# Four unused pieces of SBUF that shift the matmul operands' tiles by 128 to 192 bytes

## The chip, the cores and the metric

The kernel runs on one core of one Trainium2 chip. The metric is the device time of one execution in microseconds (us), the median of several. An execution runs one program on five engines, each with its own instruction stream: TensorE (PE in the profile; its weight loads are listed apart as PEld), VectorE (DVE), ScalarE (ACT), GpSimd (POOL) and SyncE (SP), with DMA queues that move data between device memory and SBUF. SBUF holds 128 partitions; a tile takes the same bytes, from the same start address, in each of them. A matmul reads two SBUF tiles: the weights (a block of 128 columns, loaded into the array by LDWEIGHTS) and the moving operand (up to 512 columns, streamed by MATMUL), and adds into PSUM.

## The reference, cut to what matters

A decoder trunk of two layers on 512 positions of width 1024, in float32. Layer 0 mixes with a Conformer convolution module, layer 1 with sparse attention (16 heads of 64, compressed, selected and windowed branches); each mixer is followed by a SwiGLU FFN of inner width 2816.

```
x = x + conformer_conv_module(rmsnorm(x, norm_mix[0]), ...)
x = x + swiglu_ffn(rmsnorm(x, norm_ffn[0]), ffn_w_in[0], ffn_w_out[0])
x = x + nsa_attention(rmsnorm(x, norm_mix[1]), ...)
x = x + swiglu_ffn(rmsnorm(x, norm_ffn[1]), ffn_w_in[1], ffn_w_out[1])

def swiglu_ffn(h, w_in, w_out):
    gate, up = jnp.split(h @ w_in, 2, axis=-1)
    return (jax.nn.silu(gate) * up) @ w_out
```

## The kernel before

All activations are kept transposed: eight tiles x[0..7] of 128 channels by 512 positions. Precision is kept by splitting every operand in two float32r tiles, a high part (names ending in h: hh, wh, sh, oh, ah) and the remainder (hl, wl, sl, ol, al); a product is then three matmuls, high x high, high x low and low x high.

**Projections.** `proj_start` and `proj_tile` (L396, L430) compute a tile of 128 output channels for all 512 positions: 8 blocks of the inner dimension x 3 matmuls = 24 matmuls of 512 columns, one after the other (mm3, L319 to L322; L438 to L440 where the order is fixed; the convolution's own tiles at L596). Moving operands are hh and hl (the normed input), a (the convolution's activations) or oh and ol (the attention's output); weights are wh and wl, split by ScalarE (L246) and VectorE (L268) from a raw tile wr that a DMA brought.

**FFN, first half.** The first 4 of 22 inner tiles are plain projections. The other 18 are computed in `pair` (L1200) by a scheme with seven half-size products for a 2x2 block of gate and up, in place of eight: `operand` (L1068) prepares seven combinations of the input's halves, kept split in the tiles bo (4 of them, 256 columns each for high and low), and the weights come as w1 (tiles wh, wl), or as sums in the tiles sh and sl that ScalarE and VectorE write anew in each pair (`s_part`, L1136). A product is 4 blocks; a block is three matmuls of 256 columns, or, where the combination is `WIDE`, one of 512 (high and low of the input side by side) and one of 256. Of the seven products of a pair, in their order, the weights are: wh/wl short (12 matmuls), sh/sl short (12), sh/sl long (8), sh/sl short (12), wh/wl long (8), sh/sl long (8), sh/sl long (8). All go through one line:

```
1155:                 mm = lambda out, a, b, f=False, z=False: pe(
1156:                     nc.tensor.matmul(out, a[:, k], b, start=f, stop=z, skip_group_check=True))
```

**FFN, second half.** The same scheme over the output matrix: moving operands oz, weights wh/wl or, for sums, soh and sol, which stand in the same buffers as wh and wl. The plain part of it streams ah and al.

**Attention.** Projections of q, k and v (v has the weights' columns as the moving operand, 304 or 256 wide, and hh, hl as weights, L1975), scores (L2109, L2110), transposes of the probabilities (L2155, plain float32), values (L2187), output projection.

**What sets addresses.** Tiles are cut from pools, and pools are stacked: those of the left side grow up from the bottom of SBUF, those opened with side="right" grow down from its top. A pool that is opened later starts where the earlier one of its side ends. So the start of every tile follows from the sizes of all pools below it. The pools touched: `hp` (left: hh, hl, and in the FFN the y tiles), `cp` and `ct` (right: everything of the convolution), `sw` (right: sh, sl, r22, S2 and operands' scratch of the FFN; `so`, with S, and `sb`, with bo, lie above it), `op` (right: q and later oh, ol; under it qk and kp with scores' and small tiles).

The order of instructions is partly fixed by the program and partly left to a scheduler that runs when the kernel is built.

Of the kernel before, what the change touches and what calls it, by code (L numbers as in the profile page):

```python
# [10 lines left out]
F32 = mybir.dt.float32  # L11
# [8 lines left out]
P = 128  # L20
# [121 lines left out]
def trunk(ctx: ExitStack, tc: tile.TileContext, A, out):  # L142
# [2 lines left out]
    xp = ctx.enter_context(tc.tile_pool(name="xp", bufs=1))  # L145
    wp = ctx.enter_context(tc.tile_pool(name="wp", bufs=3))
    tp = ctx.enter_context(tc.tile_pool(name="tp", bufs=2))
    hx = [ExitStack()]
    hps = [hx[0].enter_context(tc.tile_pool(name="hp", bufs=1, reuse_waits="tile"))]
    cnt = [0]  # L150

    def nm(s):
        cnt[0] += 1
        return f"{s}_{cnt[0]}"


    units = []
# [166 lines left out]
    def rsqrt(pool, a, rows, n, tag, eng=None):  # L324

        y = pool.tile([rows, n], F32, tag=tag + "y", name=nm("rsy"), bufs=1)
        t = pool.tile([rows, n], F32, tag=tag + "t", name=nm("rst"), bufs=1)
        nc.vector.tensor_scalar(t.bitcast(I32), a.bitcast(I32), 1, None, ALU.logical_shift_right)
        nc.vector.tensor_scalar(y.bitcast(I32), t.bitcast(I32), -1.0, float(0x5F3759DF), ALU.mult, ALU.add)
        for _ in range(3):  # L330
            if eng is nc.gpsimd:
                eng.tensor_tensor(t, y, y, ALU.mult)
                eng.tensor_tensor(t, t, a, ALU.mult)
                eng.tensor_scalar(t, t, -0.5, 1.5, ALU.mult, ALU.add)
                eng.tensor_tensor(y, y, t, ALU.mult)
                continue
            nc.vector.scalar_tensor_tensor(t, y, -0.5, y, ALU.mult, ALU.mult)
            nc.vector.tensor_tensor(t, t, a, ALU.mult)
            state["root"] = nc.vector.scalar_tensor_tensor(y, t, 1.5, y, ALU.add, ALU.mult)
        return y  # L340
# [9 lines left out]
    def split_hi(m, gcol):  # L350
        hh[m] = hps[0].tile([P, T], F32R, tag=f"hh{m}", name=nm(f"hh{m}"))
        parted(nc.scalar.activation(hh[m], x[m], AF.Copy, scale=v(gcol + m)))
# [121 lines left out]

    def conv_module():
        with ExitStack() as cx:
            cp = cx.enter_context(tc.tile_pool(name="cp", bufs=1, side="right"))
            ct = cx.enter_context(tc.tile_pool(name="ct", bufs=2, side="right"))
            pa = cx.enter_context(tc.tile_pool(name="pa", bufs=1, space=PSUM))
# [514 lines left out]
    def ffn(acc, gnext, layer):  # L994
# [9 lines left out]
        with ExitStack() as cx:  # L1004
# [4 lines left out]
            so = cx.enter_context(tc.tile_pool(name="so", bufs=1, side="right", reuse_waits="tile"))  # L1009
            sx = ExitStack()  # L1010
            sb = sx.enter_context(tc.tile_pool(name="sb", bufs=1, side="right", reuse_waits="tile"))
            sw = sx.enter_context(tc.tile_pool(name="sw", bufs=1, side="right", reuse_waits="tile"))
            box = {}

# [462 lines left out]
    def nsa(acc, gnext):  # L1477
        cx = ExitStack()
# [8 lines left out]
        def pool(cxx, name, bufs, **kw):  # L1487
            return cxx.enter_context(tc.tile_pool(name=name, bufs=bufs, **kw))
# [89 lines left out]
        ppx, p2x = ExitStack(), ExitStack()  # L1578
        p2 = pool(p2x, "ap2", 3, space=PSUM, reuse_waits="tile")
        px = pool(ppx, "apx", 4, space=PSUM, reuse_waits="tile")  # L1580
        op = pool(cx, "op", 1, side="right", reuse_waits="tile")
        qx = ExitStack()
        qk = pool(qx, "qk", 1, side="right", reuse_waits="tile")
        sx = ExitStack()
# [762 lines left out]
        return acc  # L2347

    acc = conv_module()
    cx0.close()  # L2350
    acc = ffn(acc, V_NM1, 0)
    acc = nsa(acc, V_NF1)
    ffn(acc, None, 1)
    hx[0].close()

# [155 lines left out]
```

## Time and profile before

| | |
|---|---|
| three runs | 1157.77, 1159.03, 1159.23 us; median 1159.03 |
| profiled execution | 1158.09 us, of which 1156.2 us span from the first to the last instruction |
| granted TensorE clock | 1.000 |
| DMA | 179.69 MB, mean 155 GB/s |

The pair loops of the two FFNs lie at 221.39 to 398.12 and 862.13 to 1038.81 us of the span. A row of the timeline gives start, duration, engine, line, operation, output<-inputs, and how many instructions are merged in it. TensorE's instructions overlap: the next starts before the one ahead ends, so what one costs is the distance of two starts, not its duration.

### The profile page before, as it was taken

Reading aid. Unit: us, or ns where it says so; the run is one execution under the profiler, and the core shown is the slowest. Engines: PE = TensorE matmul, PEld = TensorE weight load, DVE = VectorE, ACT = ScalarE, POOL = GpSimd, SP = SyncE. Lnnn points to the kernel's source line nnn. Section 1 sums busy time; section 2 is a strip of 40 time slices with the busy share of each in tenths; the row PEclk is TensorE's granted clock in tenths of the full one; section 3 lists DMA queues with packets and bytes.
Section 4 is the critical chain, followed back from the end, with each engine's and each line's share of the span. In section 5 each row is a group of like instructions: output and inputs, shape, how many; then the busy total and the mean of one; then the engine's idle time right before and its main releaser. Section 6 shows DMA issues by size and latency. Waiting matters only on the chain.

```text
span 1156.2 us, 20758 instructions
## 1 busy us (share of the span) xinstructions
PE 1148.9 (99%) x7644; PEld 990.5 (86%) x7644; DVE 949.4 (82%) x1878; ACT 639.7 (55%) x1206; POOL 306.4 (26%) x399
## 2 busy tenths in 40 slices
PE   9999999999999999999999999999999999999998
PEld 6878788899999889998779877778889999998998
DVE  6999898999999788874565988855799999987876
ACT  6666654455555454553334788863455555554543
POOL 1698101011111101110233577850001111110120
PEclk9999999999999999999999999999999999999999
DMA  9646437477777768753465211144237777776892
GB/s 361 228 116 190 119 115 214 109 183 191 190 185 192 178 196 212 153 160 91 137 162 153 60 31 36 28 130 126 92 108 176 185 187 184 183 178 169 230 197 83
DMA packets 81269, 179.69 MB, mean 155 GB/s; under 512 B 29200, under 2 KB 31120, under 8 KB 80144
## 3 DMA queue, kind: packets, MB, share of 16 engines
q1 hardware_dynamic: 56928, 105.52, 29.4%
q0 software_dynamic: 23952, 72.59, 28.1%
q8 instruction: 60, 0.98, 0.4%
q14 instruction: 41, 0.34, 0.1%
q10 hardware_dynamic: 288, 0.26, 0.1%
HBM read 163.50 MB, written 4.75 MB: 146 GB/s over the span
## 4 chain that ended last, share of the span: by engine, by line
PE 94%; DVE 3%; ACT 1%; issue 1%; DMA 0%; SPq 0%; ACTq 0%
PE st L1157 43%; PE pp L596 7%; PE pp L320 6%; PE pp L322 6%; PE pp L321 6%; PE O L2187 3%; PE T L2155 3%; PE st L321 2%; PE st L320 2%; PE st L322 2%; PE S L2109 2%; PE pv L1975 1%; PE S L2110 1%; PE pp L440 1%; PE pp L439 1%; PE pp L438 1%
## 5 line engine op out<-in xcount | busy, mean ns | idle before, releaser
L1157 PE MATMUL st<-bo,sh 128*128 128x256 f32 (+1 forms) x1008 | 259.8, 333 | 0.0
L246 ACT ACTIVATE wh<-wr 128x1024 fp32r<-128x1024 f32 (+2 forms) x143 | 148.3, 1038 | 140.6 <-issue 54.0
L268 DVE TENSOR_TENSOR wl<-wr,wh 128x1024 fp32r<-128x1024 f32 (+2 forms) x143 | 177.3, 1240 | 51.3 <-ACT wh L246 47.5
L1157 PE MATMUL st<-bo,sl 128*128 128x256 f32 x720 | 203.2, 282 | 0.0
L1157 PEld LDWEIGHTS st<-bo,sh 128*128 128x128 f32 x1008 | 170.5, 189 | 20.1
L1157 PEld LDWEIGHTS st<-bo,sl 128*128 128x128 f32 x720 | 136.6, 190 | 0.1
L1143 DVE TENSOR_TENSOR sl<-S,sh 128x512 fp32r<-128x512 f32 x144 | 93.1, 687 | 16.9 <-ACT sh L1142 16.6
L1157 PE MATMUL st<-bo,wh 128*128 128x256 f32 (+1 forms) x432 | 103.1, 316 | 0.0
L1157 PE MATMUL st<-oz,soh 128*128 128x256 f32 x512 | 88.7, 278 | 0.0
L1118 POOL DMA_DIRECT2D S<-fw_x x36 | 21.1, 588 | 241.5 <-ACT c L1172 125.8
L1142 ACT ACTIVATE sh<-S 128x512 fp32r<-128x512 f32 x144 | 82.3, 619 | 0.2
L1196 ACT ACTIVATE g<-g 128x512 f32<-128x512 f32 x36 | 22.8, 633 | 106.5 <-DVE g L1193 106.5
L1157 PE MATMUL st<-bo,wl 128*128 128x256 f32 x288 | 80.3, 279 | 0.0
L1124 POOL DMA_DIRECT2D S<-fw_x x36 | 42.6, 1184 | 136.6 <-DMA S<-fw_x 136.5
L1157 PEld LDWEIGHTS st<-oz,soh 128*128 128x128 f32 x512 | 77.9, 188 | 0.5
L320 PE MATMUL pp<-hh,wh 128*128 128x512 f32 x192 | 77.1, 401 | 0.1
L673 POOL TENSOR_TENSOR pv<-pv,tap 128x512 f32<-128x512 f32 x45 | 69.7, 1550 | 26.0 <-ACT tap L670 23.1
L1157 PEld LDWEIGHTS st<-bo,wh 128*128 128x128 f32 x432 | 70.7, 188 | 6.6
L321 PE MATMUL pp<-hl,wh 128*128 128x512 f32 x192 | 75.8, 395 | 0.0
L322 PE MATMUL pp<-hh,wl 128*128 128x512 f32 x192 | 75.7, 395 | 0.0
L2143 POOL TENSOR_SCALAR Pm<-Pm,rq,gates 128x512 f32<-128x512 f32 (+2 forms) x96 | 67.0, 708 | 33.0 <-DVE rq L2133 21.9
L1157 PE MATMUL st<-oz,sol 128*128 128x256 f32 x256 | 71.7, 280 | 0.2
(350 smaller groups left out, 2951.5 us busy)
## 6 DMA issues: line engine op xcount, KB each, us to landing
S<-fw_x POOLq DMA_DIRECT2D x72, 512.0 KB, 5.8
wr<-fw_in SPq DMA_DIRECT2D x44, 512.0 KB
So<-fw_q POOLq DMA_DIRECT2D x38, 512.0 KB, 7.3
wr<-fw_q SPq DMA_DIRECT2D x24, 512.0 KB
bd<-bands POOLq DMA_DIRECT2D x8, 1280.0 KB, 13.0
r<-fw_x SPq DMA_DIRECT2D x36, 256.0 KB
wr<-cw_in SPq DMA_DIRECT2D x14, 512.0 KB
wr<-fw_p SPq DMA_DIRECT2D x12, 512.0 KB
```

What stands on the lines that cost most here:

```text
L246: state["wh"] = parted(after(nc.scalar.activation(hi[:, :cols], raws[i][:, :cols], AF.Copy), pin.get(AF)))
L268: parted(after(nc.vector.tensor_tensor(lo[:, :cols], raws[i][:, :cols], hi[:, :cols], ALU.subtract), pin.get(ALU)))
L320: held(nc.tensor.matmul(ps, wh, xh, start=first, stop=False))
L321: held(nc.tensor.matmul(ps, wh, xl, start=False, stop=False))
L322: held(nc.tensor.matmul(ps, wl, xh, start=False, stop=last))
L596: pe(nc.tensor.matmul(ps, w[:, k * P:(k + 1) * P], z[k], start=m == 0, stop=m == len(todo) - 1))
L673: last["pool"] = pe(nc.gpsimd.tensor_tensor(dst, c, z, ALU.add))
L1124: pe(nc.gpsimd.dma_start(S[n].rearrange("p (a b) -> p a b", a=2), fw_x(n)[:, None, 2 * T:].to_broadcast([P, 2, T]), accum_op=ALU.add))
L1142: pe(nc.scalar.activation(h_[:, c], z, AF.Copy))
L1143: pe(nc.vector.tensor_tensor(l_[:, c], z, h_[:, c], ALU.subtract))
L1157: nc.tensor.matmul(out, a[:, k], b, start=f, stop=z, skip_group_check=True))
L2143: kept(nc.gpsimd.tensor_scalar(Pt, Pt, sm[:, k:k + 1], gates[:, t + k, br * 16 + h:br * 16 + h + 1], ALU.mult, ALU.mult))
```

## The change

A helper `gap` opens a pool with a single tile that nothing reads or writes. Four such pieces are put in: 128 bytes on the left ahead of `hp`, 160 bytes on the right ahead of the convolution's pools, 192 bytes on the right between `sb` and `sw` in the FFN, and 128 bytes on the right ahead of `op` in the attention.

```
+    def gap(cx, n, **kw):
+
+        cx.enter_context(tc.tile_pool(name=nm("gap"), bufs=1, **kw)).tile([P, n // 4], F32, name="gap")
...
-    hps = [hx[0].enter_context(tc.tile_pool(name="hp", bufs=1, reuse_waits="tile"))]
...
+    gap(ctx, 128)
+    hps = [hx[0].enter_context(tc.tile_pool(name="hp", bufs=1, reuse_waits="tile"))]
...
     def conv_module():
         with ExitStack() as cx:
+            gap(cx, 160, side="right")
             cp = cx.enter_context(tc.tile_pool(name="cp", bufs=1, side="right"))
...
             sb = sx.enter_context(tc.tile_pool(name="sb", bufs=1, side="right", reuse_waits="tile"))
+            gap(sx, 192, side="right")
             sw = sx.enter_context(tc.tile_pool(name="sw", bufs=1, side="right", reuse_waits="tile"))
...
+        gap(cx, 128, side="right")
         op = pool(cx, "op", 1, side="right", reuse_waits="tile")
```

No instruction is added, and every engine's instructions stand in the same order as before (the scheduled programs differ in line numbers, and in four waits on freed memory that stand at a neighbouring instruction). What changes is where tiles start. In the table, "distance" is the start of the weights that are loaded for the next product, less the start of the moving operand that is streaming meanwhile, in bytes modulo 256; blocks of weights and halves of operands are multiples of 256 bytes apart, so one number holds for a whole group.

| products (moving operand; weights) | starts modulo 256 before | after | distance before | after |
|---|---|---|---|---|
| FFN pairs (bo; sh, sl): 864 short, 432 long with 432 short | 224; 224 | 224; 32 | 0 | 64 |
| FFN pairs (bo; wh, wl) | 224; 32 | same | 64 | 64 |
| FFN second half (oz; wh, wl, soh, sol) | 224; 32 | same | 64 | 64 |
| FFN second half, plain (ah, al; wh, wl) | 224; 32 | same | 64 | 64 |
| projections (hh, hl, oh, ol; wh, wl), 1319 long | 160; 32 | 32; 32 | 128 | 0 |
| convolution's output (a; wh, wl), 192 long | 192; 32 | 32; 32 | 96 | 0 |
| scores (ks, kl; St) and (kst; St) | 224 and 192; 160 | 224 and 192; 32 | 192 and 224 | 64 and 96 |
| transposes (cc; Pm) | 160; 160 | 160; 32 | 0 | 128 |

Tiles that DMAs write shift as well where they lie in these pools (the bands of the convolution, r22, the attention's scratch); x, wr and S stay.

More of the change, by code (lines that the diff above doesn't have):

```diff
@@ L147, in trunk, with gap @@
     tp = ctx.enter_context(tc.tile_pool(name="tp", bufs=2))
+    def gap(cx, n, **kw):
+        cx.enter_context(tc.tile_pool(name=nm("gap"), bufs=1, **kw)).tile([P, n // 4], F32, name="gap")
     hx = [ExitStack()]
-    hps = [hx[0].enter_context(tc.tile_pool(name="hp", bufs=1, reuse_waits="tile"))]
     cnt = [0]
@@ L154, in nm @@
         return f"{s}_{cnt[0]}"
+    gap(ctx, 128)
+    hps = [hx[0].enter_context(tc.tile_pool(name="hp", bufs=1, reuse_waits="tile"))]
     units = []
@@ L476, in conv_module @@
         with ExitStack() as cx:
+            gap(cx, 160, side="right")
             cp = cx.enter_context(tc.tile_pool(name="cp", bufs=1, side="right"))
@@ L1011, in ffn @@
             sb = sx.enter_context(tc.tile_pool(name="sb", bufs=1, side="right", reuse_waits="tile"))
+            gap(sx, 192, side="right")
             sw = sx.enter_context(tc.tile_pool(name="sw", bufs=1, side="right", reuse_waits="tile"))
@@ L1580, in nsa @@
         px = pool(ppx, "apx", 4, space=PSUM, reuse_waits="tile")
+        gap(cx, 128, side="right")
         op = pool(cx, "op", 1, side="right", reuse_waits="tile")
```

## Prediction

> **What bounds the kernel.** I read the page first: the span, the busy times and the chain that ended last.
>
> ```profile
> span 1156.2 us, 20758 instructions
> PE 1148.9 (99%) x7644; PEld 990.5 (86%) x7644; DVE 949.4 (82%) x1878; ACT 639.7 (55%) x1206; POOL 306.4 (26%) x399
> PE 94%; DVE 3%; ACT 1%; issue 1%; DMA 0%; SPq 0%; ACTq 0%
> ```
>
> TensorE is busy for 99% of the span and is 94% of the chain, so a nanosecond saved between two products counts, if nothing else takes its place. A busy PE here only means that product follows product; how fast they follow must be read from their starts. Next the groups by form, for the products of the FFN's pair loop whose weights are the tiles sh and sl:
>
> ```profile
> L1157 PE MATMUL st<-bo,sl 128*128 128x256 f32 x720 | 203.2, 282 | 0.0
> L1157 PE MATMUL st<-bo,sh 128*128 128x512 f32 x432 | 156.1, 399 | 0.0
> L1157 PE MATMUL st<-bo,sh 128*128 128x256 f32 x576 | 106.7, 283 | 0.0
> ```
>
> The 432 long ones (512 columns) each go with one sl product, so 720 - 432 = 288 sl and 576 sh, 864 in all, stand in products of short ones only. The mean durations are modelled ends of pipelined instructions; I don't use them. The timeline of TensorE over one pair does the work (start, duration; only the first row of each of the seven products, and of the next pair, is kept):
>
> ```profile
> 239.82 0.39 PE L1157 MATMUL st<-bo,wh 128*128 128x256 f32 x2
> ...
> 241.18 0.40 PE L1157 MATMUL st<-bo,sh 128*128 128x256 f32 x2
> ...
> 242.62 0.40 PE L1157 MATMUL st<-bo,sh 128*128 128x512 f32 x1
> ...
> 244.03 0.40 PE L1157 MATMUL st<-bo,sh 128*128 128x256 f32 x2
> ...
> 245.48 0.39 PE L1157 MATMUL st<-bo,wh 128*128 128x512 f32 x1
> ...
> 246.89 0.40 PE L1157 MATMUL st<-bo,sh 128*128 128x512 f32 x1
> ...
> 248.31 0.40 PE L1157 MATMUL st<-bo,sh 128*128 128x512 f32 x1
> ...
> 249.72 0.39 PE L1157 MATMUL st<-bo,wh 128*128 128x256 f32 x2
> ```
>
> Differences of starts: the product of twelve short ones on wh/wl takes 241.18 - 239.82 = **1.36 us**; the two of the same shape on sh/sl take 1.44 and 1.45. The moving tile (bo), the PSUM target's kind, the row count and the data type are the same; what differs is the weights' tile, and by the table above its distance: 64 for wh/wl, 0 for sh/sl. That is 113 against 120 ns for each short product. The products of eight with long ones take 1.41 (wh/wl, distance 64) and 1.41, 1.42, 1.41 (sh/sl, distance 0): there the distance hardly shows.
>
> **The change, part by part.** It adds no instruction, moves none in any engine's order, and moves no DMA. Four waits for work long done go to the neighbouring instruction that uses the same freed memory; the wait lists otherwise stay. I cost that at nothing. So only starts of tiles change, and the terms are the distances in the table.
>
> *Short products of the pair loop, 0 to 64.* Per pair, two products come down from 1.44 and 1.45 to 1.36: 0.17 us. The three long products on sh/sl go from 1.41 + 1.42 + 1.41 to three times 1.41: 0.01. There are 18 pairs in each of 2 layers: 36 x 0.18 = 6.5 us; with the starts rounded to 0.01 us the sum lies between 6.1 and 6.5, and I take **-6.3 us**. It needs TensorE never to wait in these loops, and no other engine to be late:
>
> ```profile
> 221.39:398.12 176.73, 176.73 (x1218) 163.57 (x1217) 160.04 (x298) 98.13 (x195) 30.85 (x36) 1.00 0.72 182
> 862.13:1038.81 176.68, 176.68 (x1217) 163.51 (x1216) 160.01 (x298) 98.16 (x195) 30.87 (x36) 1.00 0.73 182
> ```
>
> These are the two loops (length; busy PE, weight loads, DVE, ACT, POOL; clock, DMA share, GB/s): TensorE is busy throughout at clock 1.00; VectorE works 160.04 / 18 = 8.89 us in a pair of 176.73 / 18 = 9.82. A pair of 9.82 - 0.18 = 9.64 still leaves it 0.75 us idle. What is late next is the low half wl of the next pair's weights, VectorE's last step before it is needed:
>
> ```profile
> 248.53 1.22 DVE L268 TENSOR_TENSOR wl<-wr,wh 128x1024 fp32r<-128x1024 f32 x1
> 249.83 0.19 PEld L1157 LDWEIGHTS st<-bo,wl 128*128 128x128 f32 x1
> 258.21 1.22 DVE L268 TENSOR_TENSOR wl<-wr,wh 128x1024 fp32r<-128x1024 f32 x1
> 259.73 0.19 PEld L1157 LDWEIGHTS st<-bo,wl 128*128 128x128 f32 x1
> ```
>
> wl ends at 249.75, 0.08 us ahead of its load, in the pair that also splits y of the plain part; in the next pair it ends at 259.43, 0.30 ahead. VectorE's chain starts in each pair from results of TensorE, so at worst the full 0.18 eats this margin: 0.10 lost in one pair of each layer, nothing in the others. **+0.2 us.**
>
> *Projections, 128 or 96 to 0.* 1319 products with hh, hl, oh or ol streaming, 192 in the convolution's output. A tile of 24 such products, first start to the next tile's first start:
>
> ```profile
> 198.95 0.39 PE L438 MATMUL pp<-hh,wh 128*128 128x512 f32 x1
> ...
> 204.30 0.39 PE L440 MATMUL pp<-hh,wl 128*128 128x512 f32 x1
> 204.52 0.39 PE L438 MATMUL pp<-hh,wh 128*128 128x512 f32 x1
> ...
> 781.69 0.40 PE L320 MATMUL pp<-oh,wh 128*128 128x512 f32 x1
> ...
> 787.29 0.40 PE L320 MATMUL pp<-oh,wh 128*128 128x512 f32 x1
> ...
> 152.35 0.40 PE L320 MATMUL pp<-a,wh 128*128 128x512 f32 x1
> ...
> 157.98 0.40 PE L320 MATMUL pp<-a,wh 128*128 128x512 f32 x1
> ```
>
> 5.57 and 5.60 at distance 128, 5.63 at 96. So one distance has more than one beat, and the distance isn't alone in it. Distance 0 between two long products occurs nine times, never in a run; the first and the last:
>
> ```profile
> 401.38 0.39 PE L322 MATMUL st<-ah,wl 128*128 128x512 f32 x1
> 401.61 0.39 PE L1157 MATMUL st<-bo,sh 128*128 128x512 f32 x1
> ...
> 1042.08 0.39 PE L322 MATMUL st<-ah,wl 128*128 128x512 f32 x1
> 1042.31 0.39 PE L1157 MATMUL st<-bo,sh 128*128 128x512 f32 x1
> ```
>
> 0.23 us each; the nine average 231.7 ns, which is 5.56 for a tile. That is the nearest row, so I take the best of the known beats, 5.57, for all: of the 1511 / 24 = 63 tiles, the 8 of the convolution's output gain 0.06 each, the 8 of the attention's output 0.03, and the other 47, which I put half-way between 5.57 and 5.60, 0.015: 0.48 + 0.24 + 0.70 = **-1.4 us.** The ends are wide, since nine single cases aren't a run. If distance 0 cost long products what it costs short ones, 6.7 ns, 1511 of them would lose 10 us; if it saved as much, they would gain 10. That the long pair products barely differ between 0 and 64 speaks for a small effect: the 1.42 against 1.41 is at most 2.5 ns for each long one, 1511 x 2.5 = 3.8 us either way, which I keep as the likely ends.
>
> *The rest.* The attention's transposes go from 0 to 128, its score products from 192 and 224 to 64 and 96, the V projections (some 180 of 304 or 256 columns) change among 0, 64, 128.
>
> ```profile
> L2155 PE MATMUL T<-cc,Pm 128*128 128x128 f32 x288 | 40.2, 273 | 0.0
> ```
>
> By the same 6.7 ns, the transposes bound this term at 2 us and all the others together at 2 more, on either side; I take 0, as they move both toward and away from distances that the pair loop shows to be dear. The convolution's bands and their operand move together by 160 bytes, so their distances stay.
>
> The sum is -6.3 + 0.2 - 1.4 = **-7.5 us** against the profiled execution's 1158.09, so 1150.6. The median of the three runs, 1159.03, lies 0.9 higher; on that scale the forecast is **1151.5 us**.
>
> **A rule that speaks against it.** The Trainium skill, "TensorE: Matmul & The Clock Gate", section "Step-by-step: what each phase is for", states that TensorE has two independent read ports into SBUF, one for the streaming operand and one for weights, and that loading the next weights takes no read bandwidth from the running product. By that rule no distance could matter and the sum would be 0. The rows 1.36 against 1.44 and 1.45 disagree, unless something other than the distance sets sh/sl apart; that is the first rival.
>
> **The rivals.**
> *Place, not distance.* sh and sl lie elsewhere than wh and wl, far more than 192 bytes away, and are written anew in each pair by ScalarE and VectorE while products run. If either of these makes the 0.08 us, moving them by 192 bytes brings the loops nothing: 1159.0 - 1.4 = 1157.6, or 1159.0 where the rule holds for the projections too. Against it: the summed weights of the FFN's second half are written in the same way while products run, at distance 64, and lie in wh/wl's place; the trace can't part place from distance. Chance 0.08.
> *The slow beat.* Short products also run at distance 64 in the FFN's second half, on wh/wl:
>
> ```profile
> 416.31 0.40 PE L1157 MATMUL st<-oz,wh 128*128 128x256 f32 x2
> ...
> 419.13 0.40 PE L1157 MATMUL st<-oz,wh 128*128 128x256 f32 x2
> ```
>
> 24 of them in 2.82 us, 118 ns each and not 113. So 64 allows two beats. If the sh/sl products settle into the slower one, each product of twelve takes 1.41, a pair gains 0.07, the loops 2.5 us: 1159.0 - 2.5 - 1.4 = 1155.1. Against it: the wh/wl products of the same pair hold 1.36 beside them. Chance 0.14.
> *Projections gain more.* The tile's last step above, 204.52 - 204.30, is 0.22 us; a run of 0.229 would be 5.50 a tile, and 63 tiles x 0.08 = 5.0 us: 1159.0 - 6.1 - 5.0 = 1147.9. Chance 0.10.
> *Projections lose (slower).* If long products at distance 0 lose what short ones do, 6.7 ns x 1511 = +10.1 us: 1159.0 - 6.1 + 10.1 = 1163.0. It decides from 4.1 ns a product on, where it eats the gain. For it: nothing but the short products. Against: the long pair products at 0. Chance 0.04.
> *VectorE paces the pair.* If its chain, not TensorE, holds the pair at 9.82 us, the loops gain nothing: 1159.0 - 1.4 = 1157.6. Against it: the 0.9 us that it idles in a pair. Chance 0.02.
>
> **How the numbers follow.** The forecast itself has 0.62, and by the likely ends of its projections' term (3.8 us to either side of no change) reaches from 1149.1 to 1156.7. The range of 8 in 10 reaches past the projections' larger gain below and the slow beat above: **1147.0 to 1156.5**; outside lie place, VectorE, the loss, and a little at each edge. A measurement of this kernel tells some 0.2%, 2.3 us, from no change. Faster by more: forecast, slow beat and larger gain, and a little of the rest, 0.87. Within 0.2%: place and VectorE, 0.09. Slower: 0.04.
>
> **What would show it.** In the profile after, the first rows of the seven products of a pair: all three short products at 1.36, 249.72 - 239.82 = 9.90 us from one pair to the next come down to 9.72, each of the two loops to some 173.5. 1.41 there means the slow beat, 1.44 means place. Tiles of 24 long projections: 5.56 to 5.57 if the third term is right, 5.63 and more if long products mind distance 0. A wait of weight loads for wl (L275 then) of more than 0.1 us a pair would be VectorE. The forecast is wrong if the loops keep 176.7 us, or if they shorten and the projections give it back.

## The result and the profile after

| | before | after |
|---|---|---|
| median (range) | 1158.46 us (1157.77 to 1159.23, 4 runs) | 1152.2 us (1151.8 to 1152.57, 4 runs) |
| ratio after/before | | 0.9944, 95% interval 0.9932 to 0.9957 |
| span of the profiled execution | 1156.2 us | 1150.1 us |

The time lies 0.7 us from the forecast, 1151.5. Its terms don't: the pair loops, which were to bring 6.3 us, brought 0.1, and the stretches with the projections, which were to bring 1.4, brought 5.8. That the sum fits is luck: an error of some 6 us in one term and one of some 4 in the other largely cancel. In the changed kernel L1157 has become L1166, L268 is L275, L320 to L322 are L327 to L329, and L438 to L440 are L445 to L447.

First the page after: the span, the busy times and the chain that ended last.

```profile
span 1150.1 us, 20758 instructions
PE 1141.1 (99%) x7644; PEld 989.6 (86%) x7644; DVE 948.5 (82%) x1878; ACT 639.7 (56%) x1206; POOL 306.3 (27%) x399
PE 86%; DVE 8%; ACT 2%; issue 2%; POOL 2%; DMA 1%; SPq 0%; POOLq 0%; DVEq 0%; ACTq 0%
```

Busy TensorE is down 7.8 us, the span 6.1: some new waiting has come, and VectorE's share of the chain is 8% where it was 3%. To see where, I cut both spans at the same places of the program: the first product of each pair loop, and the first plain product behind it. Before, the three stretches outside the loops (length; busy PE, weight loads, DVE, ACT, POOL; clock, DMA share, GB/s):

```profile
0.00:221.39 221.39, 218.26 (x1526) 173.83 (x1527) 198.88 (x305) 130.12 (x188) 89.18 (x89) 1.00 0.58 183
398.12:862.13 464.01, 463.20 (x2896) 384.22 (x2895) 342.56 (x823) 261.54 (x552) 144.18 (x225) 1.00 0.45 118
1038.81:1156.20 117.39, 114.00 (x794) 105.34 (x792) 87.89 (x154) 51.73 (x76) 11.28 (x13) 1.00 0.67 170
```

After, all five, in order:

```profile
0.00:218.84 218.84, 214.32 (x1526) 173.46 (x1527) 198.04 (x305) 130.22 (x188) 89.11 (x89) 1.00 0.58 185
218.84:395.51 176.67, 176.67 (x1218) 163.48 (x1217) 160.02 (x298) 98.19 (x195) 30.85 (x36) 1.00 0.73 182
395.51:856.28 460.77, 459.74 (x2897) 384.22 (x2896) 342.46 (x823) 261.52 (x552) 144.21 (x225) 1.00 0.45 119
856.28:1032.94 176.66, 176.66 (x1218) 163.48 (x1216) 160.05 (x298) 98.05 (x195) 30.88 (x36) 1.00 0.72 182
1032.94:1150.10 117.16, 113.69 (x794) 104.97 (x792) 87.89 (x154) 51.74 (x76) 11.29 (x13) 1.00 0.67 171
```

The loops changed by 0.06 and 0.02 us. The first stretch (convolution and first projections) lost 2.55, the third (attention and the projections around it) 3.24, the last 0.23: 6.1 together.

The timeline of TensorE over one pair after; as before, only the first row of each of the seven products and of the next pair is kept:

```profile
237.21 0.40 PE L1166 MATMUL st<-bo,wh 128*128 128x256 f32 x2
...
238.62 0.40 PE L1166 MATMUL st<-bo,sh 128*128 128x256 f32 x2
...
240.04 0.40 PE L1166 MATMUL st<-bo,sh 128*128 128x512 f32 x1
...
241.45 0.40 PE L1166 MATMUL st<-bo,sh 128*128 128x256 f32 x2
...
242.87 0.40 PE L1166 MATMUL st<-bo,wh 128*128 128x512 f32 x1
...
244.28 0.40 PE L1166 MATMUL st<-bo,sh 128*128 128x512 f32 x1
...
245.69 0.40 PE L1166 MATMUL st<-bo,sh 128*128 128x512 f32 x1
...
247.11 0.40 PE L1166 MATMUL st<-bo,wh 128*128 128x256 f32 x2
```

All seven products take 1.41 to 1.42 us. The two short ones on sh/sl did improve, from 1.44 and 1.45. But the short one on wh/wl, whose own distance did not change, went from 1.36 to 1.41 and gave it back: 1.36 + 1.44 + 1.45 = 4.25 before, 3 x 1.413 = 4.24 after. The pair stays at 9.90 us.

And three tiles of projections, on hh, oh and a (first row of the tile and of the next; of the first also the last product):

```profile
196.47 0.39 PE L445 MATMUL pp<-hh,wh 128*128 128x512 f32 x1
...
201.68 0.39 PE L447 MATMUL pp<-hh,wl 128*128 128x512 f32 x1
201.91 0.39 PE L445 MATMUL pp<-hh,wh 128*128 128x512 f32 x1
...
771.79 0.39 PE L327 MATMUL pp<-oh,wh 128*128 128x512 f32 x1
...
777.23 0.39 PE L327 MATMUL pp<-oh,wh 128*128 128x512 f32 x1
...
151.08 0.39 PE L327 MATMUL pp<-a,wh 128*128 128x512 f32 x1
...
156.52 0.39 PE L327 MATMUL pp<-a,wh 128*128 128x512 f32 x1
```

Each is 5.44 us, that is 226.7 ns a product, where 5.57, 5.60 and 5.63 stood before.

### The profile page after: what moved, and what is told of

It reads as the page before. It is cut to its first block, busy times and chain, and to the rows that moved or that the text cites. A ratio compares the mean times of both kernels' runs of the same rounds, so it can differ in the third digit from the quotient of the medians.

```text
span 1150.1 us, 20758 instructions
## 1 busy us (share of the span) xinstructions
PE 1141.1 (99%) x7644; PEld 989.6 (86%) x7644; DVE 948.5 (82%) x1878; ACT 639.7 (56%) x1206; POOL 306.3 (27%) x399
## 4 chain that ended last, share of the span: by engine, by line
PE 86%; DVE 8%; ACT 2%; issue 2%; POOL 2%; DMA 1%; SPq 0%; POOLq 0%; DVEq 0%; ACTq 0%
PE st L1166 44%; PE pp L327 5%; PE pp L329 5%; PE pp L328 5%; PE O L2197 3%; PE T L2165 3%; PE pp L604 3%; PE st L328 2%; PE st L327 2%; PE st L329 2%; PE S L2119 2%; DVE wl L275 2%; PE pv L1985 1%; PE S L2120 1%; POOL pv L681 1%
## 5 line engine op out<-in xcount | busy, mean ns | idle before, releaser
L1166 PE MATMUL st<-bo,sh 128*128 128x256 f32 (+1 forms) x1008 | 257.7, 331 | 0.0
L275 DVE TENSOR_TENSOR wl<-wr,wh 128x1024 fp32r<-128x1024 f32 (+2 forms) x143 | 177.6, 1242 | 50.2 <-ACT wh L253 46.8
L1166 PE MATMUL st<-bo,sl 128*128 128x256 f32 x720 | 202.3, 281 | 0.0
L1166 PEld LDWEIGHTS st<-bo,sh 128*128 128x128 f32 x1008 | 169.7, 189 | 20.0
L1166 PEld LDWEIGHTS st<-bo,sl 128*128 128x128 f32 x720 | 135.2, 188 | 0.1
L1166 PE MATMUL st<-bo,wh 128*128 128x256 f32 (+1 forms) x432 | 105.0, 320 | 0.0
L1166 PE MATMUL st<-oz,soh 128*128 128x256 f32 x512 | 88.3, 277 | 0.0
L1166 PE MATMUL st<-bo,wl 128*128 128x256 f32 x288 | 80.9, 281 | 0.0
L1166 PEld LDWEIGHTS st<-oz,soh 128*128 128x128 f32 x512 | 77.7, 188 | 0.5
L1166 PEld LDWEIGHTS st<-bo,wh 128*128 128x128 f32 x432 | 71.5, 189 | 6.7
L327 PE MATMUL pp<-hh,wh 128*128 128x512 f32 x192 | 76.1, 396 | 0.1
L329 PE MATMUL pp<-hh,wl 128*128 128x512 f32 x192 | 74.8, 391 | 0.0
L1166 PE MATMUL st<-oz,sol 128*128 128x256 f32 x256 | 71.6, 280 | 0.2
```

Source lines behind the costliest of these rows:

```text
L275: parted(after(nc.vector.tensor_tensor(lo[:, :cols], raws[i][:, :cols], hi[:, :cols], ALU.subtract), pin.get(ALU)))
L327: held(nc.tensor.matmul(ps, wh, xh, start=first, stop=False))
L329: held(nc.tensor.matmul(ps, wl, xh, start=False, stop=last))
```

## The experiments

**The pieces apart.** The first two runs take the change in two: only the piece between `sb` and `sw`, and all but this one.

```
 e1_pair_gap_only
-    gap(ctx, 128)
...
-            gap(cx, 160, side="right")
...
-        gap(cx, 128, side="right")

 e2_no_pair_gap
-            gap(sx, 192, side="right")
```

> Only the 192 bytes ahead of sh and sl; projections stay at distance 128 and 96. By the prediction's main term (short products gain by distance 64) this alone gives about -6.3 us against the kernel before, pairs at 9.72 us. By the projections' theory (all of the gain comes from long projections at distance 0) it gives 0 within 0.5 us, tiles of 24 projections stay at 5.57 to 5.60, and the pair stays at 9.89 us because its short products fall into the beat of 117.7 ns (a product of twelve at 1.41 us).

> The other three pieces without the 192 bytes: sh and sl stay at distance 0, projections go to 0. By the prediction's main term about -1.4 us against the kernel before. By the projections' theory the whole gain of the change, -6 to -6.5 us, tiles of 24 projections at 5.44 us where nothing waits, pairs at 9.89 us with products at 1.36, 1.41 and 1.44.

Measured: 1158.19 us with the pair piece alone (ratio to before 0.9998, 0.9989 to 1.0006), 1152.33 with the other three (0.9954, 0.9940 to 0.9967). The pair piece brings nothing that can be told by itself; the other three bring the whole. The first loop of each run:

```profile
221.38:397.88 176.50, 176.50 (x1217) 163.31 (x1216) 159.99 (x298) 98.09 (x195) 30.86 (x36) 1.00 0.72 182
...
218.79:395.50 176.71, 176.71 (x1217) 163.49 (x1216) 159.97 (x298) 98.16 (x195) 30.85 (x36) 1.00 0.72 182
```

The first pair of each loop in the run with the pair piece alone shows something that the loop's length hides. Here are its two short products on sh/sl, at distance 64, and the first long product behind them (second loop; L1164 is this kernel's L1157):

```profile
864.13 0.39 PE L1164 MATMUL st<-bo,sh 128*128 128x256 f32 x2
...
865.49 0.39 PE L1164 MATMUL st<-bo,sh 128*128 128x256 f32 x2
...
866.85 0.39 PE L1164 MATMUL st<-bo,wh 128*128 128x512 f32 x1
```

Both take 1.36 us, the price that the prediction gave them. With the long products the pair goes over to 353 ns for a block of 768 columns, and all later products of the loop take 1.41. So sh/sl at 64 can have the predicted price; it doesn't keep it in a pair that mixes short and long products.

**The plain products too.** In the FFN's second half the plain products (ah, al) stand at 64. Two more pieces bring 190 of them to 0.

```
 e3_plain_at_0
+            gap(cx, 192, side="right")
             fp = cx.enter_context(
+            gap(cx, 64, side="right")
             ft = cx.enter_context(
```

> The change, and 192 more bytes ahead of ah and al (with 64 behind them, so that all other tiles of the FFN keep their start modulo 256): the plain part of the FFN's second half goes from distance 64 to 0. If long products run at 226.7 ns at distance 0 wherever they stand, its some 290 products come down from 233.3 to 226.7: -1.9 us against the change. If the beat of 226.7 belongs to the projections and not to the distance, 0.

Measured: 1151.73 us (0.9944, 0.9931 to 0.9956), the change's own ratio. The plain products fell from 233.3 to 230.3 ns on average; those at 0 reach 227 only after some products: behind the pair products that stand among them, from 400.5 us on, the first seven take 228, 231, 231, 236, 228, 232 and 231 ns and the next ones 227. Meanwhile the mean short product rose from 116.5 to 116.9 ns. From the first plain product of the second half to its last product, the two layers together take 226.2 us in the change's trace and in this one: nothing was left of the 1.2 us.

**Is it the long products that hold the slow beat?** After the change all of a pair runs at 353 ns for a block (768 columns: 3 x 117.8, or 235.3 + 118), while the wh/wl short product of before had 340. This run computes each long product as two short ones, so that nothing long is left in the loops.

```
 e4_short_only
-                    mm(ps[:, :2 * H], wh, o.rearrange("p a b -> p (a b)"), first)
+                    mm(ps[:, :H], wh, o[:, 0], first)
+                    mm(ps[:, H:2 * H], wh, o[:, 1])
```

> The change, with each long product of the FFN's pairs and second half written as two short ones of 256 columns (one more weight load, the same columns, the same sums). If long products at distance 64 are what puts the short ones beside them into the slow beat, all blocks run at 3 x 113.3 = 340 ns, a pair takes 7 x 1.36 = 9.52 us in place of 9.89, and the loops gain 36 x 0.37 = 13 us. If something outside TensorE paces the pair at 9.89 us (it is 9.89 in the kernel before and after), or if the slow beat is the one that short products at 64 fall into whatever stands before them, the pair stays at 9.89.

```profile
218.89:395.56 176.67, 176.67 (x1502) 176.66 (x1500) 159.97 (x298) 98.04 (x195) 30.85 (x36) 1.00 0.73 182
```

With 284 more matmuls in the first loop (x1502 for x1218) it has the same length to 0.01 us, 1152.98 us in all (0.9959, 0.9946 to 0.9973). Every block is at 353 ns. The long products aren't needed to hold the slow beat; it lasts among short ones alone. The fast one does so too: in the second half of this run's first FFN, behind a stall, 116 short products in a row at distance 64 take 113.3 ns each, from 442.8 to 455.9 us. The loops of this run are entered in the slow beat, as those of the change are; what short products alone would bring when the loop is entered in the fast one wasn't tried, so the 13 us of the expectation are not ruled out.

**Other distances in the pair loops.** The pieces around `bo` are set by layer so that wh/wl and sh/sl have one distance, the same for both; three runs give six distances. One of them as a diff:

```
 s2_pairs_192_and_96
+            if (128, 32)[layer]:
+                gap(sx, (128, 32)[layer], side="right")
             sb = sx.enter_context(
...
-            gap(sx, 192, side="right")
+            if (64, 160)[layer]:
+                gap(sx, (64, 160)[layer], side="right")
```

> The change, but all products of the pair loop (wh, wl as well as sh, sl) at one distance: 0 in layer 0, 128 in layer 1. If the distance sets the beat: at 0 short products at 120 ns (products of twelve at 1.44 us) and long ones, as in the projections, free of loss while their weights load; at 128 something else than 9.89 us a pair. If something outside TensorE paces the pair, 9.89 in both layers wherever the distance allows it.

> As before with 192 in layer 0 and 96 in layer 1. If the distance sets the beat, pairs differ between the layers and from 9.89 us; a distance at which short products run at 113.3 ns and long ones at 226.7 would give pairs of 9.52. If the pair is paced from outside, 9.89 or more.

> As before with 32 in layer 0 and 160 in layer 1; the same two readings.

One run each: 1154.27, 1150.34 and 1152.42 us. The loops of the first two of these runs, distances 0, 128, 192 and 96:

```profile
218.84:396.83 177.99, 177.99 (x1217) 164.82 (x1216) 160.36 (x298) 98.18 (x195) 30.85 (x36) 1.00 0.72 181
858.60:1035.28 176.68, 176.68 (x1218) 164.45 (x1216) 159.92 (x298) 98.02 (x195) 30.88 (x36) 1.00 0.73 182
...
218.85:395.57 176.72, 176.72 (x1217) 163.77 (x1216) 159.94 (x298) 98.12 (x195) 30.85 (x36) 1.00 0.73 182
856.51:1031.50 174.99, 174.99 (x1217) 163.01 (x1216) 159.69 (x298) 98.03 (x195) 30.86 (x36) 1.00 0.73 184
```

Distances 32 and 160 gave 176.78 and 177.17. The loops go from 175.0 to 178.0 us with the starts alone, so no other engine paces the pair at 9.89: VectorE's work is 160 us in all of them. That before and after agree at 176.7 is a coincidence of two sums. Distance 96 is the one that gains, 9.79 us a pair. Nor does the start of one operand alone set the price: at distance 0 the short products on sh/sl take 1.44 us with both tiles at 224 modulo 256 (before) and with both at 32 (the first layer here, with 0), and at distance 96 the last two long products of a pair take 1.39 with bo at 192 (the second layer here, with 96) and with bo at 224 (the last run below). For the projections the weights stand at 32 in every run, so there the distance can't be told from the start of the moving tile.

**96 in both layers**, without and with the pieces for the plain products.

```
 b1_pairs_96
+            gap(sx, 32, side="right")
             sb = sx.enter_context(
-            gap(sx, 192, side="right")
+            gap(sx, 160, side="right")

 b2_pairs_96_plain_0
+            gap(cx, 192, side="right")
             fp = cx.enter_context(
+            gap(cx, 64, side="right")
             ft = cx.enter_context(
```

> The change, with gaps of 32 and 160 bytes around bo in place of the 192, so that both layers' pair loops run at distance 96 for wh/wl and for sh/sl. Theory (the pair's period follows the distance of the two operands, whichever layer): both layers at 9.79 us a pair as layer 1 was with 96 before, 36 x 0.10 = 3.6 us under the change, 1152.2 - 3.6 = 1148.6 us. Rival (layer 1's loop was shorter for a reason of its own): layer 0 stays at 9.89, 1150.3 us. Rival (the change's 9.89 is set by another engine): 1152.2.

> As the run with both loops at 96, and the plain products of the FFN's second half moved from 64 to 0 too. Theory: 190 long products lose 233.4 - 227 = 6.4 ns each, 1.2 us, of which the neighbouring short products gave 0.7 back when this was tried at pairs of 64: 1148.1 us against 1148.6 for the loops alone. Rival: the giving back is as large as the gain, no difference.

```profile
218.99:393.99 175.00, 175.00 (x1218) 163.02 (x1216) 159.89 (x298) 98.17 (x195) 30.85 (x36) 1.00 0.73 184
854.80:1029.78 174.98, 174.98 (x1217) 162.99 (x1216) 159.71 (x298) 98.02 (x195) 30.88 (x36) 1.00 0.73 184
```

Measured: 1148.75 us (0.9917, 0.9902 to 0.9932) and 1148.75 us (0.9914, 0.9900 to 0.9929). Layer 0 does as layer 1 did, and the two loops give 1.7 us each. This beats both kernels, the change by some 3.4 us. The plain products bring nothing that can be told here either.

**Projections at another distance.** The pieces ahead of `hp` and of `op` are 64 bytes in place of 128, which puts hh, hl at distance 64 and oh, ol at 192; the convolution's output stays at 0.

```
 p64_projections_64
-    gap(ctx, 128)
+    gap(ctx, 64)
...
-        gap(cx, 128, side="right")
+        gap(cx, 64, side="right")
```

> The change, with 64 in place of 128 bytes ahead of hp and ahead of op: the projections of hh and hl go to distance 64, the attention's output projection to 192, the convolution's output stays at 0, the pair loops stay as in the change. Theory (0 itself is the cheap distance for long products): those at 64 take 233.3 ns as the plain products of the FFN do, 5.60 us a tile, 1319 x 6.5 = 8.6 us lost again less some waits that go: about 1159 to 1160 us. Rival (any move away from 128 would have brought it): 5.44 a tile and 1152 us. Where 192 comes out between 5.44 and 5.60 is open.

A tile on oh at 192 and one on hh at 64, as starts of the tile and the next:

```profile
780.64 0.39 PE L327 MATMUL pp<-oh,wh 128*128 128x512 f32 x1
...
786.13 0.39 PE L327 MATMUL pp<-oh,wh 128*128 128x512 f32 x1
...
849.32 0.40 PE L445 MATMUL pp<-hh,wh 128*128 128x512 f32 x1
...
854.92 0.40 PE L445 MATMUL pp<-hh,wh 128*128 128x512 f32 x1
```

5.49 us at 192 and 5.60 at 64: the beats follow the distance, and 0 is the cheapest of the five seen for long products (0, 64, 96, 128, 192). In all 1156.25 us (0.9980, 0.9971 to 0.9990). That is some 3 us better than expected: the output projection had been counted at the price of 64 and took 5.49, which is 0.8 us in its 8 tiles, and the late starts of the projections of hh and hl came down by some 2.5 us, the waits for wl among them, which are told of below and were down to 0.2 us. The convolution's output kept its 5.44, as expected.

**What chooses between 340 and 353 at distance 64.** Behind the first matmul of each pair's wh/wl short product, layer 0 gets one product with zeros, layer 1 two; they add zero to the same sum.

```
 z1_break_before_short
                     mm(ps[:, :H], wh, o[:, 0], first)
+                    if first and isinstance(w, tuple) and mark[0]:
+                        for _ in range(1 + layer):
+                            pe(nc.tensor.matmul(ps[:, :P], zb, zb, start=False, stop=False, skip_group_check=True))
                     mm(ps[:, :H], wh, o[:, 1])
```

> The change, with zero products of 128 columns (bfloat16, added into the same sum) behind the first block's first matmul of each pair's wh/wl short product: one in layer 0, two in layer 1. They cost some 54 x 0.06 to 0.12 = 3 to 6 us. Theory (at distance 64 the slow beat is handed on from product to product until something interrupts it, and the product after an interruption runs in the fast beat): the first short product, less its interrupted block, falls from 353 to 340 ns a block, and the sh/sl short one behind it too. Rival (the beat is set by what the operands are and where they lie, not by what ran before): both stay at 353.

The timeline of this kernel in layer 0, and behind the gap in layer 1 (L1175 is the zero product):

```profile
257.03 0.28 PE L1168 MATMUL st<-bo,wh 128*128 128x256 f32 x1
257.15 0.23 PE L1175 MATMUL st<-zb 128*128 128x128 bf16 x1
...
257.51 0.39 PE L1168 MATMUL st<-bo,wh 128*128 128x256 f32 x2
...
258.53 0.39 PE L1168 MATMUL st<-bo,sh 128*128 128x256 f32 x2
...
259.89 0.39 PE L1168 MATMUL st<-bo,sh 128*128 128x512 f32 x1
...
925.72 0.29 PE L1175 MATMUL st<-zb 128*128 128x128 bf16 x2
...
926.14 0.40 PE L1168 MATMUL st<-bo,wh 128*128 128x256 f32 x2
...
927.20 0.40 PE L1168 MATMUL st<-bo,sh 128*128 128x256 f32 x2
...
928.61 0.39 PE L1168 MATMUL st<-bo,sh 128*128 128x512 f32 x1
```

Behind one zero product the three remaining wh/wl blocks take 258.53 - 257.51 = 1.02 us, 340 ns each, and the sh/sl product of twelve behind them 259.89 - 258.53 = **1.36**, the price that the prediction gave it, in all 18 pairs. Then long products come and the beat is 353 again. Behind two zero products the same blocks take 1.06 and the same product 1.41, in every pair of layer 1 but the first. The same operands at the same addresses thus run at either beat. So what ran just before decides, and an interruption by itself isn't enough. (The first pair of layer 1 comes from a projection and not from a pair; it had 1.36 behind two zero products. One and two zero products were tried in different layers only, not exchanged.) The run took 1155.47 us (one run): the zero products cost more than the beat brings.

**Does a change of distance interrupt?** The last run puts 160 in place of the change's 192: sh/sl at 96, wh/wl still at 64.

```
 f1_sums_96_direct_64
-            gap(sx, 192, side="right")
+            gap(sx, 160, side="right")
```

> The change with 160 bytes in place of 192 between sb and sw: sh/sl go to distance 96, wh/wl stay at 64. Theory (at 64 the slow beat is handed on along a run of products at one distance; a change of distance ahead of a product interrupts it): the wh/wl short product, which now follows sh/sl long ones at 96, is back at 1.36 us; sh/sl short at 1.41, sh/sl long at 1.39, wh/wl long at 1.41: 1.36 + 2 x 1.407 + 3 x 1.393 + 1.41 = 9.76 us a pair, 36 x 0.13 = 4.7 us under the change, 1147.5 us. Rival (the change of distance is no interruption; wh/wl short have the slow beat whenever no product at 0 stands before them): 9.81 us a pair, 1149.3 us.

The wh/wl short product of this kernel, with the long one on sh/sl ahead of it and the short one behind:

```profile
314.30 0.39 PE L1166 MATMUL st<-bo,sh 128*128 128x512 f32 x1
315.68 0.40 PE L1166 MATMUL st<-bo,wh 128*128 128x256 f32 x2
...
317.10 0.40 PE L1166 MATMUL st<-bo,sh 128*128 128x256 f32 x2
```

It takes 1.42 us; the theory said 1.36 and has fallen in this form. Coming from long sh/sl products at 96 the product is slow, coming from those at 0, before the change, it was fast. Distance 0 ahead isn't a rule either: after the change the first pair of both loops follows projections at 0, and its wh/wl short product takes 1.41 us. The kernel is as good as 96 for all: 1149.02 us (0.9918, 0.9905 to 0.9932), as its rival had said (1149.3). The rival's rule, slow whenever no product at 0 stands ahead, doesn't hold as it stands: the first pairs with only the pair piece follow projections at 128 and are fast.

## Why the prediction was right in its time and wrong in its terms

*What bounds the kernel*: right. TensorE was the bound before and after, and every gain is a shorter interval between two of its products.

*Short products of the pair loop, 0 to 64, -6.3 us*: **wrong, 0 in its place.** The step that failed is "per pair, two products come down from 1.44 and 1.45 to 1.36". It read 1.36 as the price of distance 64. It was the price of 64 for a product that is entered in the fast beat, as the wh/wl product was before, behind long products on sh/sl at 0. With all of the pair at 64 the fast beat doesn't outlast the pair's long products: in the runs of that kind 22 pairs began in it (19 with zero products, 2 with the pair piece alone, 1 with the projections at 64), and each went over to 353 ns a block at its long products. The rival of the slow beat had the price for sh/sl right, 1.41. But it kept wh/wl at 1.36, as the argument against it did ("the wh/wl short products of the same pair hold 1.36 beside them"), and so expected 2.5 us from the loops. A product whose operands hadn't moved changed with its neighbours: that was in neither. *Place, not distance* is out, since the loops' length changed over a range of 3 us with the distance, with moves of a few hundred bytes; so is *VectorE paces the pair*, by the same runs.

*Wait for wl, +0.2 us*: nothing of it in the loops, where busy and length are equal, as nothing got shorter there. The same wait came where it wasn't looked for, in the plain projections ahead of the loops. VectorE's wl there is late for a TensorE that now runs faster. The waits of TensorE's weight loads (us in all, times, longest), before and after:

```profile
PEld pp L440 <- DVE wl L268: 0.5, 2, 0.2
...
PEld pp L447 <- DVE wl L275: 1.4, 2, 0.7
```

*Projections, 128 or 96 to 0, -1.4 us*: **mis-sized.** The rival of a larger gain had the mechanism, and 5.50 a tile; a tile took 5.44. The step that was off is the choice of the value: nine single cases at 0 averaged 231.7 ns, but stood between products of other kinds and said little of a run, which has 226.7. The run with the plain products at 0 shows how that misleads: 228 to 236 ns for the first seven behind products of another kind, and some 227 for those that follow. Counted over all starts of the traces, the long products that follow each other within 245 ns sum to 4.4 us less in the first stretch (751 of them, from 233.0 to 227.2 ns) and 4.1 less in the third (some 1015, from 232.8 to 229.0, among them products that did not move to 0). Of these 8.5 us some 2.6 went again: 1.9 in longer late starts, the waits for wl among them, and 0.7 in the other products. The rest is the 5.8 us of the two stretches. The one wait of the loops that the prediction priced was thus a wait of the projections, and larger.

*The rule on two independent read ports* ("TensorE: Matmul & The Clock Gate", section "Step-by-step: what each phase is for" in the Trainium skill) would have given no change. The traces disagree: tiles on oh that differ in nothing but starts take 5.44, 5.49 and 5.60 us at distances 0, 192 and 128. Which of the two reads is held up, the traces don't show.

*The rest, 0*: the last stretch gave 0.23 us, and nothing in the attention stands out beyond the 0.7 us above: the 288 transposes, moved from 0 to 128, take 32.3 us by their starts before and after.

What selects the beat at one distance isn't settled. Shown is that it can be either with the same operands, that either lasts from product to product among short ones, that the fast one ended at the long products of a pair at 64, that one zero product in a pair's first block brought the fast one and two didn't, and that it came out slow behind 96. A longer series of interruptions of graded length would be the next step, and a loop of short products alone that is entered in the fast beat another; neither was tried.

## What to carry to other kernels

Where TensorE is busy throughout, list the intervals between starts of matmuls by shape and by the distance of weights and moving operand modulo 256; a few bytes of padding may shorten a long run (here 2.9% of each projection tile, from 5.60 to 5.44). A price read off one product in a mixed sequence belongs to that sequence: move neighbours, and an untouched product may change as much as the moved one. Measure a run of the new kind before multiplying a single case, and try several distances, since the best one for the pair loops' mix of short and long products (96) wasn't the best for long ones in a run (0).

## What was not expected of the hardware

The steady beats differ by distance, and at 64 there are two for short products. Long products in a run: 226.7 ns at distance 0, 228.9 at 192, 233.3 at 64, 232 to 233.3 at 128, 234.3 at 96. Short products at 64: 113.3 or 117.8 ns. 226.7 is twice 113.3, and no steady run of these products went below it. The Trainium skill ("TensorE: Matmul & The Clock Gate", section "Back-to-back issue gap") gives the columns by 2.4 GHz plus 2.5 ns for one isolated product, 215.8 ns for 512 columns. This kernel's bfloat16 products of zeros (warm<-zb, from 127.4 us after the change, weights loaded for each) agree, with 215 to 217 ns from start to start at a granted clock of 1.00; behind no product of 512 columns of the projections and the FFN was the next start less than 224 ns away.

Both beats of one distance also stand in a single kernel without any edit. In the FFN's second half after the change, short products at 64 take 2.83 us for 24 early on and 2.72 later, behind a wait for sol of 0.3 us. That isn't a rule: at 1124.3 us of the same trace the short products on soh and sol go from 113.3 to 117.8 ns behind a single start that is 0.1 us late. The rows of the first case:

```profile
413.71 0.40 PE L1166 MATMUL st<-oz,wh 128*128 128x256 f32 x2
...
416.54 0.40 PE L1166 MATMUL st<-oz,wh 128*128 128x256 f32 x2
...
445.00 0.39 PE L1166 MATMUL st<-oz,soh 128*128 128x256 f32 x2
...
447.72 0.39 PE L1166 MATMUL st<-oz,soh 128*128 128x256 f32 x2
```
